# Sliding attention with its values two steps behind its scores, and three pairs of experts combined late for the second half of the tokens

## Chip, cores and metric

One core of a Trainium2 chip runs one program. The metric is the device time of one execution in microseconds (us). PE is TensorE (matmuls; PEld its weight loads), DVE is VectorE, ACT is ScalarE, POOL is GpSimd, SP is the engine that issues the DMAs here.

## The reference, cut to what matters

Two transformer blocks run one after the other on 512 tokens of width 1024, all in float32. The first mixes a convolution branch with sliding-window attention and ends with a mixture of experts; its output is normalised, and the second block begins with another normalisation.

```python
# first block
conv_o = conformer_conv(u_conv, ...) @ w_conv_out            # 31 taps per channel
attn   = sliding_window_attention(q, k, v, sinks)            # blocks of 128 queries, window 128
    scores = einsum(q, [k of block before, k of block]) * 64**-0.5 - slopes * rel
    p   = exp(scores - m);  p = p / (sum(p) + exp(sink - m));  out = einsum(p, v)
h = x + (sigmoid(gc) * conv_o + sigmoid(ga) * (attn @ w_attn_out)) @ w_out
h = h + hierarchical_moe(rms_norm(h, g_ffn), ...)            # 32 experts, 2 per token
x = rms_norm(h, g_final)
# second block
proj = rms_norm_2(x, mix_norm_gain) @ w_in_2                 # then gated delta rule, sparse attention, FFN
```

## The kernel before, in words

The program is written with tile pools. Each engine's order comes from a planner that goes by the order of the program text where it can and fills in other ready work; instructions made through `pe` (L1154) keep the text's order on PE, and `issue_after` puts an engine's instructions behind a given one. There are 20 big buffers of 8 KB a partition (`ck`, L181) and 8 PSUM banks (`ps`, L178). Float32 products are made of a high and a low part (`hilo`, L331), so a projection of one 128-column weight tile is 24 matmuls (`mm3`, L323). A weight tile is split into its parts by ACT (L196) and by POOL or DVE in turn (L214).

**Sliding attention** (`swa`, L671) goes through 8 steps, one for each block of 128 queries (`qb`) and each half of the heads (`r2`). `scores` (L681) makes the products on PE (L692), adds the bias on DVE (L694), takes the maximum (L696 to L698), lets ACT do the exponentials (L700, L702), sums (L703, L704), and scales on ACT (L706). `values` (L709) turns the result on PE (L717), copies it on ACT (L719) and multiplies by V (L722); after a block's second half, `hilo` writes the block's columns of `ath`, `atl` (L335, L336). Values of a step follow the scores of the next step. `weave` (L1368) puts one piece of `fill` after each `yield`: 20 half projections of 12 matmuls each, which are the last queries, the last convolution channel and six gate tiles (their tanh is L664). Beside it the convolution's taps (L572 on DVE, one chain a channel) are handed out four at a time by `pump`. After the attention comes `branch(ath, atl)` (L621), which reads all blocks.

**The experts** (`moe`, L983) go by 16 pairs `i`. For each: gate, turning of the pair before, half of `combine` of pair i-2, up, the rest of `combine`, and `down` of pair i-1, which writes its result to the one buffer `self.y` as high and low part (L339, L340). `combine` (L1214) multiplies by a one-hot matrix for each of 4 token tiles and 2 halves, two matmuls each, and DVE adds the result to `h` (L1225). At pair 15 a branch (`overflow`, L1057) is passed, which all engines skip here.

**The end of the first block** (`block2`, L1278): after pair 15's `combine` of a tile, `done` squares it on ACT (L1287), multiplies it by a gain (`gained`, L1291: DVE for tiles 0 and 1, POOL for 2 and 3), and squares it again. `pair` (L1293) makes the two norms' roots for two tiles at once (L1297 to L1304, root at L388) and scales each tile (L1307). `turn` (L368) transposes a tile on PE (L374) and splits it (L335, L336). `begin(2)` (L284) starts two projections on the first 256 tokens as soon as tiles 0 and 1 are turned; `finish` does the other 256. The second block (`phase_b`, L1347) takes these from `begun`. Weight tiles are prepared ahead by `fill_w` (L249), which keeps `1 + look` of them ready; `look` is 2 here.

Of the kernel before, what the change touches and what calls it, by code (L numbers as in the profile page):

```python
# [15 lines left out]
P = 128  # L16
S = 512
D = 1024
# [134 lines left out]

AHEAD = 11


class Net:
# [513 lines left out]
    def swa(self, q, kv, ath, atl):  # L671
# [9 lines left out]
        def scores(qb, r2):  # L681
            nk = 128 if qb == 0 else 256
            k0 = max(qb - 1, 0) * P
            s = self.small([P, 4, 256], "sc", bufs=2)
            mx, nmx, sm, es = (self.small([P, 4], n) for n in ("mx", "nmx", "sm", "es"))
# [41 lines left out]

        steps = [(qb, r2) for qb in range(NT) for r2 in range(2)]
        prev = None
        for st in steps:  # L730
            s = scores(*st)
            yield
            if prev is not None:
                values(*prev)
                yield
            else:
                for _ in range(3):
                    yield
            prev = st + (s,)
        values(*prev)  # L740

# [241 lines left out]
    def moe(self):  # L983

        quad, hms, ys = self.quad, {}, {}
        self.gather_first()
        self.weights()
        self.prefetch(AHEAD)
        for i in range(16):
            q = quad[i // 2]  # L990
            back = self.combine(quad[i // 2 - 1], i % 2, ys.pop(i - 2)) if i > 1 else iter(())
            if i % 2 == 0:
                g = self.gather(i // 2 + 1, quad) if i < 14 else iter(())
                next(g, None)
                self.gather_back(i // 2, quad)
            gate = self.experts("w_gate", i, q)
            if i:
                hT = self.turned(hms.pop(i - 1))
            for _ in range(2):
                next(g, None)  # L1000
            for _ in range(4):
                next(back, None)
            hms[i] = self.gated_up(gate, self.experts("w_up", i, q))
            if i % 2 == 0:
                quad[i // 2]["back"]()
            for _ in back:
# [11 lines left out]
        self.block2(quad.pop(7), y)  # L1018

# [173 lines left out]

    def down(self, i, hT, q):

# [3 lines left out]
        for jj in range(2):  # L1199
# [7 lines left out]
            self.prefetch(self.used + AHEAD)  # L1207
        y = self.y
        for half in range(2):
# [3 lines left out]

    def combine(self, q, j, y, done=None):  # L1214

        nc = self.nc
        mm = nc.tensor.matmul
        for t in range(NT):
            for half in range(2):
                fs = slice(half * 512, half * 512 + 512)  # L1220
                pc = self.ps()
                l = q["ohT"][:, j, t * P:(t + 1) * P]
                self.pe(mm, pc, l, y[:, 0, fs], start=True, stop=False)
                self.pe(mm, pc, l, y[:, 1, fs], start=False, stop=True)
# [52 lines left out]

    def block2(self, q, y):  # L1278

# [9 lines left out]
        def gained(t):  # L1289
            e = nc.gpsimd if t > 1 else nc.vector  # L1290
            e.tensor_tensor(out=self.h[:, t], in0=self.h[:, t], in1=self.rows[:, 0], op=ALU.mult)  # L1291

        def pair(t2):  # L1293

            s, v_, r_ = ss[t2], v[t2], r[t2]
            iv = self.small([P, 2], "iv")
# [16 lines left out]
        def done(t):  # L1313
            if t > 1:
                with self.tc.issue_after(first[0].ins):
                    squares(t, 0)
                gained(t)
                return
# [17 lines left out]
        for t in (2, 3):  # L1336
# [846 lines left out]
```

## Time and profile before

| | |
|---|---|
| median of 3 runs | 1784.6 us (1783.42 to 1784.62) |
| the profiled execution | 1785.45 us, of which the span is 1783.7 us |
| mean granted PE clock | 0.985 |
| PE busy | 1716.4 us (96%), 8672 matmuls |
| DVE, ACT, POOL busy | 827.6 (46%), 561.3 (31%), 332.4 us (19%) |
| attention, from its first scores to the first `branch` | 75.65 to about 172.5 us |
| experts | about 345 to 818 us |
| end of the first block, to the end of `finish` | 818 to 850 us |

The span runs from the first to the last instruction of the profiled execution; the rest of its time lies around it. Times in the rows are microseconds from the start of the span. A matmul's recorded end is modelled, so matmuls of one stream overlap: their step from start to start is what they cost. A clock of 1.00 is 2.4 GHz and 0.50 is 1.2 GHz.

### The profile page before, as it was taken

The page shows a single profiled execution, that of the slowest core. Times are in us where ns is not written, and L with a number is a line of the kernel's source. Part 1 is how long each engine was busy: PE and PEld are TensorE (multiplying, and loading weights), DVE is VectorE, ACT ScalarE, POOL GpSimd, SP SyncE. Part 2 cuts the span into 40 slices and gives each one's busy share as a digit, 9 for nine tenths or more (in the row PEclk, how much of TensorE's full clock was granted, in tenths as well). Part 3 has the DMA queues.
Part 4 walks back from the last instruction along what each step waited for, and adds up shares of the span by engine and source line. Part 5 has one row for each costly group of instructions (what it writes and reads, how often), then busy time and mean ns, then how long its engine had stood idle before and what let it go on. Part 6 is the DMA issues. An engine that isn't in the chain of part 4 may idle for free.

```text
span 1783.7 us, 21733 instructions
## 1 busy us (share of the span) xinstructions
PE 1716.4 (96%) x8672; PEld 1224.0 (69%) x8672; DVE 827.6 (46%) x1516; ACT 561.3 (31%) x1052; POOL 332.4 (19%) x208
## 2 busy tenths in 40 slices
PE   8998999999999999997999999899999899999998
PEld 6866888644444454434769988776578788888886
DVE  6996365723242333237576224556835422232222
ACT  4355254310101010104662234434523322332331
POOL 1000000000000000003327312321124133333450
PEclk9998999999999999998999999999999999999999
DMA  6221326599999999992311011210123233331431
GB/s 228 71 71 24 118 95 236 213 414 384 424 425 422 427 425 426 425 375 69 99 47 36 25 64 46 72 56 25 48 71 130 71 118 94 95 95 48 142 106 48
DMA packets 131594, 303.70 MB, mean 170 GB/s; under 512 B 5757, under 2 KB 90493, under 8 KB 106402
## 3 DMA queue, kind: packets, MB, share of 16 engines
q1 hardware_dynamic: 131490, 302.28, 45.1%
q8 instruction: 70, 1.15, 0.3%
q14 instruction: 34, 0.28, 0.0%
HBM read 300.16 MB, written 2.10 MB: 169 GB/s over the span
## 4 chain that ended last, share of the span: by engine, by line
PE 44%; DVE 5%; ACT 3%; issue 3%; POOL 1%; DVEq 0%; ACTq 0%; POOLq 0%
PE ps L327 8%; PE ps L328 8%; PE ps L329 8%; PE ps L2121 3%; PE ps L2120 3%; PE ps L2119 3%; PE ps L1607 1%; PE ps L1621 1%; PE ps L1156 1%; PE ps L1623 1%; PE ps L1926 1%; PE ps L1921 1%; PE ps L1903 1%; PE ps L1829 1%; DVE ck L1492 1%
## 5 line engine op out<-in xcount | busy, mean ns | idle before, releaser
L327 PE MATMUL ps<-ck,ck 128*128 128x512 f32 (+2 forms) x1112 | 438.0, 395 | 5.3 <-ACT ck L196 2.7
L328 PE MATMUL ps<-ck,ck 128*128 128x512 f32 (+2 forms) x1112 | 429.3, 387 | 1.1 <-DVE ck L336 1.1
L329 PE MATMUL ps<-ck,ck 128*128 128x512 f32 (+2 forms) x1112 | 427.4, 385 | 0.5 <-POOL ck L214 0.5
L327 PEld LDWEIGHTS ps<-ck,ck 128*128 128x128 f32 (+1 forms) x1112 | 210.2, 189 | 60.5 <-issue 10.2
L328 PEld LDWEIGHTS ps<-ck,ck 128*128 128x128 f32 (+1 forms) x1112 | 210.5, 189 | 48.3 <-issue 7.8
L329 PEld LDWEIGHTS ps<-ck,ck 128*128 128x128 f32 (+1 forms) x1112 | 210.4, 189 | 42.8 <-issue 1.5
L1156 PE MATMUL ps<-ck,ck 128*64 128x512 f32 x1024 | 226.3, 594 | 0.0
L214 POOL TENSOR_TENSOR ck<-ck,ck 128x512 fp32r<-128x512 f32 (+1 forms) x81 | 141.9, 1768 | 357.8 <-ACT ck L196 225.4
L1156 PEld LDWEIGHTS ps<-ck,ck 128*64 128x64 f32 x1024 | 72.0, 137 | 142.1 <-issue 135.8
L214 DVE TENSOR_TENSOR ck<-ck,ck 128x512 fp32r<-128x512 f32 (+1 forms) x109 | 110.8, 1036 | 91.1 <-PE ps L2120 44.2
L2119 PE MATMUL ps<-ck,ck 128*128 128x512 f32 x304 | 119.8, 395 | 0.0
L2121 PE MATMUL ps<-ck,ck 128*128 128x512 f32 x304 | 118.5, 390 | 0.0
L2120 PE MATMUL ps<-ck,ck 128*128 128x512 f32 x304 | 118.4, 390 | 0.0
L1156 PE MATMUL ps<-ck,hT 128*64 128x512 f32 x512 | 115.0, 602 | 2.0 <-PEq L1062 2.0
L1138 POOL TENSOR_TENSOR ohw<-oh,wt 128x512 f32<-128x512 f32 x16 | 16.5, 1050 | 470.2 <-issue 334.4
L214 POOL TENSOR_TENSOR ck<-wf,ck 128x1024 fp32r<-128x1024 f32 x28 | 77.3, 2791 | 143.4 <-ACT ck L196 143.4
L339 ACT ACTIVATE ck<-ps,ws 128x512 fp32r<-128x512 f32 x32 | 21.9, 687 | 253.9 <-PE ps L1156 253.9
L196 ACT ACTIVATE ck<-ck 128x1024 fp32r<-128x1024 f32 (+1 forms) x98 | 87.0, 911 | 13.7 <-PE ps L1921 4.2
L1156 PEld LDWEIGHTS ps<-ck,hT 128*64 128x64 f32 x512 | 36.4, 138 | 72.9 <-issue 63.0
L572 DVE SCALAR_TENSOR_TENSOR ck<-ck,wdw,ck 128x495 f32<-128x495 f32 (+23 forms) x120 | 83.8, 730 | 0.3
L1225 DVE TENSOR_TENSOR h<-h,ps 128x512 f32<-128x512 f32 x128 | 79.6, 678 | 6.9 <-PE ps L1156 6.9
L2051 DVE TENSOR_TENSOR sf<-ps,sf 128x512 f32<-128x512 f32 x22 | 15.2, 691 | 127.6 <-PE ps L329 127.6
(398 smaller groups left out, 2232.3 us busy)
## 6 DMA issues: line engine op xcount, KB each, us to landing
ck<-in_w_down SPq DMA_DIRECT2D x74, 1024.0 KB, 9.4
ck<-in_w_gate SPq DMA_DIRECT2D x64, 1024.0 KB, 11.2
ck<-in_w_up SPq DMA_DIRECT2D x64, 1024.0 KB, 9.3
ck<-in_w_in SPq DMA_DIRECT2D x34, 1024.0 KB, 5.1
wf<-in_w_gate_up SPq DMA_DIRECT2D x42, 512.0 KB, 4.8
ck<-in_w_out SPq DMA_DIRECT2D x8, 1024.0 KB, 4.9
h<-in_x SPq DMA_DIRECT2D x4, 512.0 KB, 6.5
ck<-in_w_in SPq DMA_DIRECT2D x4, 512.0 KB, 7.7
```

The costliest lines, as they stand in the source:

```text
L196: nc.scalar.activation(out=h, in_=src, func=AF.Copy)
L214: e.tensor_tensor(out=out, in0=src, in1=h.bitcast(F32), op=ALU.subtract)
L327: mm(ps, wh[:, k], xh[:, k, cols], start=k == 0, stop=False, skip_group_check=part)
L328: mm(ps, wh[:, k], xl[:, k, cols], start=False, stop=False, skip_group_check=part)
L329: mm(ps, wl[:, k], xh[:, k, cols], start=False, stop=k == K - 1, skip_group_check=part)
L339: nc.scalar.activation(out=h, in_=src, func=AF.Copy, scale=scale)
L572: nc.vector.scalar_tensor_tensor(out=y[:, c, o:], in0=v[:, c, :512 - o], scalar=wdw[:, c, 30 - o:31 - o], in1=y[:, c, o:], op0=ALU.mult, o ...
L1156: return self.tc.keep_in_program_order(f(*args, **kw))
L1225: nc.vector.tensor_tensor(out=self.h[:, t, fs], in0=self.h[:, t, fs], in1=pc, op=ALU.add)
L2119: mm(acc[t], ah[:, kk, ts], wh[:, k], start=kk == 0, stop=False)
L2120: mm(acc[t], ah[:, kk, ts], wl[:, k], start=False, stop=False)
L2121: mm(acc[t], al[:, kk, ts], wh[:, k], start=False, stop=kk == K - 1)
```

## The change

`values` of a step now come after the scores of the step after the next, and the buffer `sc` for scores has three copies instead of two. After the first step's scores four fill pieces stand as before; the last two steps of values have one fill piece between them.

The pairs 13, 14 and 15 are combined at once only for token tiles 0 and 1. Pairs 13 and 15 get result buffers of their own, and after pair 15's tiles 0 and 1 all three pairs are combined for tiles 2 and 3: six matmuls into one PSUM bank and one DVE addition for each half tile. `gained` of tiles 2 and 3 moves from POOL to DVE and behind the turning of tiles 0 and 1. `pair` computes the second norm's argument with fewer small operations. `begin` starts four projections instead of two.

```diff
+LAST = (13, 14, 15)
 def swa:
-            s = self.small([P, 4, 256], "sc", bufs=2)
+            s = self.small([P, 4, 256], "sc", bufs=3)
-        prev = None
-        for st in steps:
+        behind = deque()
+        for st in [(qb, r2) for qb in range(NT) for r2 in range(2)]:
             s = scores(*st)
             yield
-            if prev is not None:
-                values(*prev)
+            if len(behind) == 2:
+                values(*behind.popleft())
+            yield
+            if not any(st):
                 yield
-            else:
-                for _ in range(3):
-                    yield
-            prev = st + (s,)
-        values(*prev)
+                yield
+            behind.append(st + (s,))
+        values(*behind.popleft())
+        yield
+        values(*behind.popleft())
 def moe:
-            back = self.combine(quad[i // 2 - 1], i % 2, ys.pop(i - 2)) if i > 1 else iter(())
+            back = self.combine(quad[i // 2 - 1], i % 2, ys[i - 2], range(2 if i - 2 in LAST else NT)) if i > 1 else iter(())
-                ys[i - 1] = self.down(i - 1, hT, quad[(i - 1) // 2])
+                ys[i - 1] = self.down(i - 1, hT, quad[(i - 1) // 2], self.ck([P, 2, D], F32R) if i - 1 == 13 else self.y)
-        for _ in self.combine(quad[7], 0, ys.pop(14)):
+        for _ in self.combine(quad[7], 0, ys[14], range(2)):
             pass
-        y = self.down(15, hT, quad[7])
+        ys[15] = self.down(15, hT, quad[7], self.ck([P, 2, D], F32R))
+    def combine_all(self, pairs, tiles, done=None):
+        for t in tiles:
+            for half in range(2):
...
+                for i, (l, y) in enumerate(pairs):
+                    for part in range(2):
+                        self.pe(mm, pc, l[:, t * P:(t + 1) * P], y[:, part, fs], start=i + part == 0, stop=part == 1 and i == len(pairs) - 1)
                 nc.vector.tensor_tensor(out=self.h[:, t, fs], in0=self.h[:, t, fs], in1=pc, op=ALU.add)
 def block2:
-            e = nc.gpsimd if t > 1 else nc.vector
-            e.tensor_tensor(out=self.h[:, t], in0=self.h[:, t], in1=self.rows[:, 0], op=ALU.mult)
+            nc.vector.tensor_tensor(out=self.h[:, t], in0=self.h[:, t], in1=self.rows[:, 0], op=ALU.mult)
-            nc.vector.reciprocal(out=iv, in_=v_[:, 0])
-            ts_(out=v_[:, 1], in0=s[:, 1], scalar1=1.0 / D, scalar2=None, op0=ALU.mult)
-            nc.vector.tensor_tensor(out=v_[:, 1], in0=v_[:, 1], in1=iv, op=ALU.mult)
-            ts_(out=v_[:, 1], in0=v_[:, 1], scalar1=EPS, scalar2=None, op0=ALU.add)
+            ev = self.small([P, 2], "ev")
+            ts_(out=ev, in0=v_[:, 0], scalar1=EPS, scalar2=None, op0=ALU.mult)
+            nc.vector.scalar_tensor_tensor(out=v_[:, 1], in0=s[:, 1], scalar=1.0 / D, in1=ev, op0=ALU.mult, op1=ALU.add)
-            r12 = self.small([P, 2], "r12")
-            nc.vector.tensor_tensor(out=r12, in0=r_[:, 0], in1=r_[:, 1], op=ALU.mult)
+            r12 = r_[:, 1]
-        for _ in self.combine(q, 1, y, done=done):
+        for _ in self.combine(quad[7], 1, ys[15], range(2), done=done):
+            pass
+        for _ in self.combine_all([(quad[i // 2]["ohT"][:, i % 2], ys[i]) for i in LAST], range(2, NT), done=done):
             pass
...
+        with self.tc.issue_after(last[1].ins):
+            for t in (2, 3):
+                gained(t)
-        finish = self.begin(2)
+        finish = self.begin(4)
```

## Rows read from the trace of the kernel before

**Rows 1.** Busy time by stretch: PE, PEld, DVE, ACT, POOL, clock, DMA share, GB/s.

```profile
75.00:162.40 87.40, 79.94 (x380) 54.68 (x378) 83.01 (x157) 45.44 (x130) 0.00 (x0) 0.94 0.17 49
162.40:172.50 10.10, 9.36 (x41) 6.74 (x42) 0.77 (x2) 3.39 (x7) 0.00 (x0) 0.83 0.46 104
125.00:150.00 25.00, 20.04 (x91) 12.83 (x90) 23.49 (x44) 13.78 (x36) 0.00 (x0) 0.80 0.08 26
150.00:175.00 25.00, 22.59 (x107) 15.83 (x106) 11.70 (x25) 14.39 (x38) 0.00 (x0) 0.93 0.19 43
172.00:200.00 28.00, 28.00 (x125) 23.21 (x124) 8.40 (x13) 9.76 (x14) 0.00 (x0) 1.00 0.25 77
```

**Rows 2.** PE's wait for scaled scores, 70 to 190 us: in total, times, longest.

```profile
PE ps L717 <- ACT sc L706: 7.5, 3, 4.3
```

**Rows 3.** Timeline of the attention: start, duration, engine, line [idle before <- releaser].

```profile
115.00 1.14 PE L692 MATMUL ps<-ck,ck 64*128 64x256 f32 x8
...
125.67 1.28 DVE L694 SCALAR_TENSOR_TENSOR sc<-ps,ck 128x512 f32<-128x512 f32 x2
...
131.54 0.60 ACT L664 ACTIVATE sg<-ps 128x512 f32<-128x512 f32 x1 [4.84 <-PE ps L329]
...
134.22 0.16 DVE L703 TENSOR_TENSOR sm<-sm,es 128x4 f32<-128x4 f32 x1 [0.99 <-ACT es L702]
...
135.78 1.67 PE L717 MATMUL ps<-ident,sc 128*128 128x128 f32 x4 [4.28 <-ACT sc L706]
...
162.31 0.17 DVE L704 RECIPROCAL sm<-sm 128x4 f32<-128x4 f32 x1
...
168.91 0.69 DVE L336 TENSOR_TENSOR ck<-ps,ck 128x512 fp32r<-128x512 f32 x1 [6.43 <-ACT ck L335]
...
172.59 0.60 ACT L664 ACTIVATE sg<-ps 128x512 f32<-128x512 f32 x1 [3.71 <-PE ps L329]
```

**Rows 4.** Timeline of PE from 778 to 850 us.

```profile
779.11 2.12 PE L1156 MATMUL ps<-ck,ohT 128*128 128x512 f32 x8
781.15 7.09 PE L1156 MATMUL ps<-ck,ck 128*64 128x512 f32 x32
...
813.39 0.49 PE L1156 MATMUL ps<-ck,ohT 128*128 128x512 f32 x1
...
827.54 1.97 PE L374 MATMUL ps<-ident,ck 128*128 128x128 f32 x8 [9.20 <-DVE ck L1307]
830.83 1.97 PE L374 MATMUL ps<-ident,ck 128*128 128x128 f32 x8 [1.32 <-DVE ck L1307]
832.72 0.61 PE L327 MATMUL ps<-ck,ck 128*36 128x256 f32 x2
...
840.40 2.13 PE L374 MATMUL ps<-ident,ck 128*128 128x128 f32 x16
```

**Rows 5.** Busy time by stretch, columns as in the first group.

```profile
837.00:840.40 3.40, 3.40 (x30) 3.37 (x29) 2.82 (x10) 2.44 (x3) 0.00 (x0) 1.00 0.00 0
```

**Rows 6.** Timeline of DVE and POOL from 814 to 846 us.

```profile
819.21 1.22 DVE L1291 TENSOR_TENSOR h<-h,ck 128x1024 f32<-128x1024 f32 x1
...
821.68 0.16 DVE L1299 TENSOR_SCALAR b_v<-b_ss 128x2 f32<-128x2 f32 x1
...
824.05 5.64 POOL L1291 TENSOR_TENSOR h<-h,ck 128x1024 f32<-128x1024 f32 x2 [114.77 <-ACT ck L1287]
824.17 6.60 DVE L1307 SCALAR_TENSOR_TENSOR ck<-h,r,ck 128x1024 f32<-128x1024 f32 x2
...
838.84 2.48 DVE L1307 SCALAR_TENSOR_TENSOR ck<-h,r,ck 128x1024 f32<-128x1024 f32 x2
```

**Rows 7.** SP's waits from 700 to 860 us, and DMA issues from 740 to 860 us.

```profile
SPq L1811 <- DVE ck L1307: 39.8, 1, 39.8
...
ck<-in_w_in SPq DMA_DIRECT2D x5, 1024.0 KB, 8.3
```

**Rows 8.** PE's waits after 850 us: in total, times, longest.

```profile
PE ps L1537 <- DVE grow L1468: 1.6, 1, 1.6
```

More of the change, by code (lines that the diff above doesn't have):

```diff
@@ L726, in values @@
                 self.hilo(po.pop(qb).rearrange("p (r q) -> p r q", r=4), ath[:, :, qs], atl[:, :, qs])
-        steps = [(qb, r2) for qb in range(NT) for r2 in range(2)]
-        prev = None
-        for st in steps:
+        behind = deque()
+        for st in [(qb, r2) for qb in range(NT) for r2 in range(2)]:
             s = scores(*st)
             yield
-            if prev is not None:
-                values(*prev)
+            if len(behind) == 2:
+                values(*behind.popleft())
+            yield
+            if not any(st):
                 yield
-            else:
-                for _ in range(3):
-                    yield
-            prev = st + (s,)
-        values(*prev)
+                yield
[3 more added lines that the diff above has]
+        values(*behind.popleft())
     def conv_norm(self, y, total):
@@ L1011, in moe @@
             if i:
-                ys[i - 1] = self.down(i - 1, hT, quad[(i - 1) // 2])
+                ys[i - 1] = self.down(i - 1, hT, quad[(i - 1) // 2], self.ck([P, 2, D], F32R) if i - 1 == 13 else self.y)
         hT = self.turned(hms.pop(15))
-        for _ in self.combine(quad[7], 0, ys.pop(14)):
+        for _ in self.combine(quad[7], 0, ys[14], range(2)):
             pass
-        y = self.down(15, hT, quad[7])
+        ys[15] = self.down(15, hT, quad[7], self.ck([P, 2, D], F32R))
         self.start_b()
-        self.block2(quad.pop(7), y)
+        self.block2(quad, ys)
     def weights(self):
@@ L1192, in turned, with down @@
         return hT
-    def down(self, i, hT, q):
+    def down(self, i, hT, q, y):
         nc = self.nc
@@ L1207, in down @@
             self.prefetch(self.used + AHEAD)
-        y = self.y
         for half in range(2):
@@ L1212, in down, with combine @@
         return y
-    def combine(self, q, j, y, done=None):
+    def combine(self, q, j, y, tiles, done=None):
+        return self.combine_all([(q["ohT"][:, j], y)], tiles, done)
+    def combine_all(self, pairs, tiles, done=None):
         nc = self.nc
         mm = nc.tensor.matmul
-        for t in range(NT):
+        for t in tiles:
             for half in range(2):
@@ L1221, in combine @@
                 pc = self.ps()
-                l = q["ohT"][:, j, t * P:(t + 1) * P]
-                self.pe(mm, pc, l, y[:, 0, fs], start=True, stop=False)
-                self.pe(mm, pc, l, y[:, 1, fs], start=False, stop=True)
+                for i, (l, y) in enumerate(pairs):
+                    for part in range(2):
+                        self.pe(mm, pc, l[:, t * P:(t + 1) * P], y[:, part, fs], start=i + part == 0, stop=part == 1 and i == len(pairs) - 1)
                 nc.vector.tensor_tensor(out=self.h[:, t, fs], in0=self.h[:, t, fs], in1=pc, op=ALU.add)
@@ L1276, in misc_w, with block2 @@
         return w[:, 0], w[:, 1]
-    def block2(self, q, y):
+    def block2(self, quad, ys):
         nc = self.nc
@@ L1289, in gained @@
         def gained(t):
-            e = nc.gpsimd if t > 1 else nc.vector
-            e.tensor_tensor(out=self.h[:, t], in0=self.h[:, t], in1=self.rows[:, 0], op=ALU.mult)
+            nc.vector.tensor_tensor(out=self.h[:, t], in0=self.h[:, t], in1=self.rows[:, 0], op=ALU.mult)
         def pair(t2):
             s, v_, r_ = ss[t2], v[t2], r[t2]
-            iv = self.small([P, 2], "iv")
             ts_(out=v_[:, 0], in0=s[:, 0], scalar1=1.0 / D, scalar2=EPS, op0=ALU.mult, op1=ALU.add)
-            nc.vector.reciprocal(out=iv, in_=v_[:, 0])
-            ts_(out=v_[:, 1], in0=s[:, 1], scalar1=1.0 / D, scalar2=None, op0=ALU.mult)
-            nc.vector.tensor_tensor(out=v_[:, 1], in0=v_[:, 1], in1=iv, op=ALU.mult)
-            ts_(out=v_[:, 1], in0=v_[:, 1], scalar1=EPS, scalar2=None, op0=ALU.add)
+            ev = self.small([P, 2], "ev")
+            ts_(out=ev, in0=v_[:, 0], scalar1=EPS, scalar2=None, op0=ALU.mult)
+            nc.vector.scalar_tensor_tensor(out=v_[:, 1], in0=s[:, 1], scalar=1.0 / D, in1=ev, op0=ALU.mult, op1=ALU.add)
             self.rsqrt(v_, r_)
-            r12 = self.small([P, 2], "r12")
-            nc.vector.tensor_tensor(out=r12, in0=r_[:, 0], in1=r_[:, 1], op=ALU.mult)
+            r12 = r_[:, 1]
             for u in range(2):
@@ L1316, in done @@
                     squares(t, 0)
-                gained(t)
                 return
```

## The prediction

> **What bounds the kernel now.** I read the busy times by stretch first. From 75 to 162.4 us PE and DVE are both nearly full: PE 79.94 and DVE 83.01 of 87.40 us [rows 1]. The reader should see two things there. DVE has only 87.40 - 83.01 = 4.39 us of idle time, and once its work there is done it has 0.77 us of work in the next 10.1 us [rows 1]. So PE waits in this stage for an engine that has little room itself.
>
> Then PE's waits: 7.5 us in three waits, all of values (L717) for scaled scores (L706) [rows 2]. PE also ran part of the time at 1.2 GHz. A granted clock of 0.80 over 25 us is 10 us at half speed, so 5.0 us of work lost; 0.93 over the next 25 us loses 1.75 us [rows 1]. Idle and slow clock together are 7.5 + 6.75 = 14.2 us. That is the most the attention part can give.
>
> The timeline of the attention shows why the scores come late. PE finished the scores of step 4 (counted from 0) at about 116.1 us, and DVE took them up at 125.67 us, behind convolution taps. ACT then held their exponentials behind the tanh of a gate tile that PE finished at 131.5 us, DVE waited 0.99 us for them, and PE, with nothing else in its order, stood 4.28 us until 135.78 [rows 3].
>
> At the end of the experts PE is the bound: pair follows pair without a gap, 8 matmuls of `combine` taking 2.04 us from start to start (779.11 to 781.15) [rows 4]. Pair 15's combine begins at 813.39; call this E. Behind it comes a chain on ACT and DVE in which PE has nothing to do. It stands 9.20 us until tile 0 is scaled (827.54) and 1.32 us until tile 1 (830.83), `begin` starts at 832.72, and tiles 2 and 3 are turned at 840.40 [rows 4].
>
> **The attention, part by part.** No instruction is added or removed; each `values` moves behind one more step of scores and two fill pieces. A fill piece is 12 matmuls at 28.00 / 125 = 0.224 us, so 2.7 us [rows 1]. With the scores' 1.14 us [rows 3] that is 2 x 2.7 + 1.1 = 6.5 us of PE work in place of a wait of at most 4.3. The last two steps of values get one piece (2.7 us) more ahead of them, not two.
>
> What is late next is DVE. The last softmax's reciprocal ends at 162.48 (L704), and PE's order cannot bring that forward by itself [rows 3]. From L704's start to the end of the last low part (168.91 + 0.69 = 169.60) the chain through ACT, PE, ACT, PE, ACT and DVE takes 7.3 us. The first `branch` started only at 172.5, when the last gate tile was done (its tanh at 172.59) [rows 3]. After the change only one fill piece (2.7 us) is left for these 7.3 us, and it fits into the chain's pauses. With L704 unmoved, `branch` therefore starts at 169.6: a gain of 2.9 us. That is the lower end. If L704 also moves forward by all of DVE's 4.39 us of idle time, the gain is 7.3. The upper end is the 14.2 us of a PE that never waits, for which DVE would have to put the last softmax ahead of taps.
>
> I take 2.9 + three quarters of 4.39 = **6.2 us**. The idle spot I can trace (0.99 us) comes from exponentials queued behind a tanh, and both move when PE runs ahead. I leave a quarter because PE will now wait for the last steps instead and may run slowly after that. The third `sc` copy keeps the old slack, since the scores that reuse a buffer still come right after the values that free it. Nothing on SP or POOL is moved here.
>
> **The experts' end.** Pairs 13 and 14 lose the combining of two tiles each: 2 x 8 matmuls, 2 x 2.04 = 4.1 us off PE while PE is the bound. The same 16 matmuls come back behind E, into PE's idle time. Of 12 DVE additions 8 disappear; they lay beside PE work and count nothing. The new result buffers take two of the 20 `ck` buffers when few loads are left; I count that at nothing, since the last loads keep 18 buffers; the price if that cover is gone is a rival below.
>
> Behind E, in the old trace's times: `gained` of tile 1 ran at 819.21 after an addition for tile 2; without that it starts about 0.6 us sooner, and so does the second square. From there to L1307 the old chain took 821.68 to 824.17, 2.5 us; two small operations, the final product and interleaved additions go, which leaves about 1.5 us. L1307 then starts near 822.6 [rows 6].
>
> The largest term is POOL. L1307 of tiles 0 and 1 took 6.60 us for two, starting 0.12 us after POOL's `gained` of tiles 2 and 3 (5.64 us); the same two operations for tiles 2 and 3 took 2.48 us without POOL beside them [rows 6]. With `gained` off POOL I take 2.48: a gain of 4.1. Tile 1 is scaled at 822.6 + 2.5 = 825.1 instead of 830.8, so its turning and `begin` start **5.7 us** earlier, at 827.0 instead of 832.72.
>
> `begin(4)` has 96 matmuls of 256 columns. The first 48 took 832.72 to 840.40, 7.7 us, partly at 1.2 GHz; I keep that, because PE still idles before them (its work behind E ended at 827.54 - 9.20 = 818.3 and now ends 4.1 us later, at 822.4, short of tile 0's scaling). The other 48 cost 48 x 3.40 / 30 = 5.4 us [rows 4, 5]. So `begin` ends at 827.0 + 7.7 + 5.4 = 840.1, just when tiles 2 and 3 were turned before, but with 5.4 us more of projection done. I count **5.4 us** from E on. Tiles 2 and 3 (`gained` now on DVE, 2 x 1.22, one square, 1.5 of small operations, 2.48 of L1307) follow the last low part near 828.8 and end near 837: 3 us of slack. If PE's clock does not fall, up to 2.5 us more; if POOL collides again, 4.1 less (below).
>
> The second block then gets three convolution channels at once, and its short gate chain has less PE work over it. That chain already cost PE 1.6 us in one wait [rows 8]. Between nothing and 4 us I take a loss of **1.5 us**, the size of that wait.
>
> **Sum.** -6.2 - 4.1 - 5.4 + 1.5 = -14.2 us. The profiled execution took 1785.45 (span 1783.7), which would become 1771.3; it lies 0.85 above the median of 1784.6, from which I get **1770.4 us**.
>
> **The rivals.**
> A. *POOL collides all the same.* With `gained` gone, POOL takes the subtraction halves of the next weight tiles (L214) earlier, and they can lie beside L1307 of tiles 0 and 1. It depends on where ACT's copies (L196) land, before or after the squares of tile 2. The 4.1 us come back: 1774.5.
> The Trainium skill ("SBUF — State Buffer", Who interferes with whom) states that a DVE instruction with two SBUF inputs and a POOL operation that reads SBUF shut each other out, the later one blocking wholly. Any POOL operation reading SBUF would do that by this rule, so moving one away helps only if no other takes its place; the pair of times above agrees with it.
>
> B. *DVE and ACT hold the attention.* The wait moves to the last two steps of values, with a slow clock after it, and L704 does not move. For it speaks that DVE is fuller than PE [rows 1]. The gain there is 2.9 or less; with 1 us, the whole is 1784.6 - (14.2 - 5.2) = 1775.6.
>
> C. *Both gains are given back downstream.* The loads keep pace with PE through the experts, and in the second block the shorter cover over the gate chain turns into waits. Against it: PE waits little there [rows 8]. Result about 1783.
>
> D. *Slower: ACT waits for a third weight chunk.* `begin(4)` asks for five weight tiles besides the small one, because two stay ahead; the fifth needs the third 1 MB chunk of the second block's weights. Before, SP stood 39.8 us behind a load (L1811) that waited for L1307 of tile 3, and such a chunk landed 8.3 us after issue [rows 7]. If the planner keeps the chunk behind that load, it lands about 8 us after the last L1307. ACT's copy of it, if put ahead of the high parts (L335) of tiles 2 and 3, holds them, and PE behind them. It decides from a landing later than about 840 in the old times. At old time 860 (20 us) the whole is 1790. Against it: the product r12, for which that load waited, is gone, and buffers are free after E.
>
> **How the numbers follow.** The forecast has 0.56, A 0.18, B 0.13, C 0.08, D 0.05. A measurement of this kernel tells about 0.2%, 3.6 us, from no change. Forecast, A and B are faster by more than that (0.87), C is the same (0.08), D slower (0.05). The forecast's own range runs from all upper ends short of the PE-bound attention (-7.3 - 4.1 - 7.9, nothing lost: 1765.3) to 2.9 of the attention with 4 us lost (1776.2). A and B both at once give 1779.7. I let the range reach from 1763, where part of DVE's taps yield to the last softmax, to 1779.
>
> **What would show it.** Attention: L717's waits near 135 us gone, a wait left at the last two steps, the first `branch` near 166 instead of 172.5, the clock above 0.8 from 125 to 150. Experts' end: 24 matmuls right after pair 15's first 8, L1307 at 1.2 to 1.3 us each, PE's wait for tile 0 near 2 instead of 9.2 us, four projections before tile 2 is turned. L1307 at 3 us beside L214 would show A, L704 near 162 would show B, an ACT copy waiting for a weight DMA ahead of L335 would show D. The prediction is wrong if the planner reorders work elsewhere by more than these terms.

## The result, and the profile after

The changed kernel takes 1776.01 us (median of 5, 1773.22 to 1776.99) against 1784.6 us; the ratio is 0.9949 with a 95% interval of 0.9935 to 0.9962, so 9.1 us less (6.8 to 11.6) by the ratio and 8.6 by the medians. The forecast was 1770.4, 14.2 us less, in a range from 1763 to 1779. The direction was right and the time lies in the range, but 5 of the 14.2 us did not come. The execution in the profile below took 1773.22 us (span 1771.4), 2.8 less than the median; from now on runs are therefore compared by ratio, and a stage by several profiles.

Lines of the changed file stand some lower than in the one before: L572 (the taps) has become L573, L694 L695, L704 L705, L717 L718, L1156 L1160, L1225 L1232, L1291 L1297, L1307 L1311, L214 L215.

**The attention.** Busy time by stretch of the changed kernel, columns as in [rows 1] (PE, PEld, DVE, ACT, POOL, granted clock, DMA share, GB/s):

```profile
75.00:162.40 87.40, 82.82 (x410) 57.46 (x410) 82.59 (x157) 48.77 (x137) 0.00 (x0) 0.96 0.23 61
162.40:172.50 10.10, 10.10 (x46) 8.32 (x46) 3.72 (x5) 2.79 (x5) 0.00 (x0) 1.00 0.07 14
125.00:150.00 25.00, 22.84 (x118) 15.13 (x114) 25.00 (x50) 19.32 (x53) 0.00 (x0) 1.00 0.06 11
150.00:175.00 25.00, 22.70 (x101) 16.42 (x101) 11.31 (x19) 11.25 (x27) 0.00 (x0) 0.86 0.29 74
75.00:154.62 79.62, 75.05 (x376) 52.73 (x375) 79.62 (x153) 45.09 (x129) 0.00 (x0) 0.98 0.26 67
```

PE's waits there, 60 to 190 us (in total, times, longest), and the rows of the timeline around them (start, duration, engine, line, idle before and its releaser):

```profile
PE ps L723 <- ACT PT L720: 2.2, 1, 2.2
PE ps L718 <- ACT sc L707: 2.0, 1, 2.0
```

```profile
148.97 1.53 PE L718 MATMUL ps<-ident,sc 128*128 128x128 f32 x4 [2.01 <-ACT sc L707]
...
152.71 1.12 PE L723 MATMUL ps<-PT,ck 128*64 128x256 f32 x4 [2.21 <-ACT PT L720]
...
154.62 0.17 DVE L705 RECIPROCAL sm<-sm 128x4 f32<-128x4 f32 x1
...
164.71 0.60 ACT L665 ACTIVATE sg<-ps 128x512 f32<-128x512 f32 x1 [2.11 <-PE ps L330]
```

The reader should see three things. The waits near 135 us are gone, and the clock of 125 to 150 us is 1.00 instead of 0.80. Two waits, 4.2 us, are left at the values of the last steps, with a clock of 0.86 around them. And DVE has no idle time at all before the last softmax: 79.62 busy of 79.62. Its reciprocal came 7.7 us earlier (154.62 instead of 162.31), the last gate tile's tanh 7.9 (164.71 instead of 172.59).

**The experts' end.** PE from 764 to 835 us, and under it ACT, then DVE and POOL:

```profile
764.80 7.04 PE L1160 MATMUL ps<-ck,ck 128*64 128x512 f32 x32
771.77 0.66 PE L1160 MATMUL ps<-ident,hm 128*128 128x128 f32 x4
773.69 0.49 PE L1160 MATMUL ps<-ck,ohT 128*128 128x512 f32 x1 [1.26 <-ACT ck L340]
774.47 2.94 PE L1160 MATMUL ps<-ck,ohT 128*128 128x512 f32 x7 [0.29 <-DVE ck L341]
777.34 7.81 PE L1160 MATMUL ps<-ck,ck 128*64 128x512 f32 x32
...
805.04 0.49 PE L1160 MATMUL ps<-ck,ohT 128*128 128x512 f32 x1
805.83 7.95 PE L1160 MATMUL ps<-ck,ohT 128*128 128x512 f32 x31 [0.29 <-DVE ck L341]
816.76 3.42 PE L375 MATMUL ps<-ident,ck 128*128 128x128 f32 x16 [2.98 <-DVE ck L1311]
832.48 2.20 PE L375 MATMUL ps<-ident,ck 128*128 128x128 f32 x16 [0.20 <-DVE ck L1311]
```

```profile
771.91 0.60 ACT L1184 ACTIVATE sil<-ps 128x512 f32<-128x512 f32 x1 [25.66 <-PE ps L1160]
772.46 0.60 ACT L347 ACTIVATE hT<-ps 128x512 f32<-128x512 f32 x1
772.95 1.26 ACT L340 ACTIVATE ck<-ps,ws 128x512 fp32r<-128x512 f32 x2
```

```profile
815.42 2.48 DVE L1311 SCALAR_TENSOR_TENSOR ck<-h,b_r,ck 128x1024 f32<-128x1024 f32 x2
...
816.87 5.60 POOL L215 TENSOR_TENSOR ck<-ck,ck 128x1024 fp32r<-128x1024 f32 x2 [18.41 <-ACT ck L197]
...
828.00 2.40 POOL L215 TENSOR_TENSOR ck<-ck,ck 128x1024 fp32r<-128x1024 f32 x1 [5.54 <-ACT ck L197]
828.26 2.16 DVE L394 TENSOR_TENSOR nt<-b_r 128x4 f32<-128x4 f32 x1
```

In [rows 4], 8 matmuls of `combine` follow pair 15's gate matmuls and the turning of pair 14 without a gap (779.11). Here PE stands 1.26 and 0.29 us for pair 13's result, and the 40 matmuls that follow run in part at half speed (2.94 for 7, and 7.81 us for 32 where 7.09 is usual). ACT wrote that result at 772.95, 8 us after its matmuls had ended (764.8): ACT has the write queued behind pair 15's gate (L1184), whose matmuls ended at 771.8. The new buffer comes out of the weights' rotation. That the buffer was still being read until then was my first explanation; a run below tests whether the buffer is the cause, and the loads behind that run show that its readers are not. So pair 15's combine (E) starts at 805.04, 8.35 us earlier than before, of which 6.93 was there already at 763 us.

Behind E the forecast's picture holds: the scaling of tiles 0 and 1 takes 2.48 us for both instead of 6.60, PE waits 2.98 us for tile 0 instead of 9.20, and when tiles 2 and 3 come, four projections lie behind PE, which has stood still for 0.20 us only. From 820 to 950 us PE's wait for L1468's row (now L1476) is 1.6 as in [rows 8], and one is new:

```profile
PE ps L1545 <- DVE grow L1476: 1.6, 1, 1.6
PE ps L1506 <- POOL s L1505: 1.4, 1, 1.4
```

**Stage by stage.** Start times of eight instructions in the timelines, in us, as shifts against the first profile of before. The rows are ACT's first copy of keys and values (L587 before the change), ACT's copy of the convolution norm's mean (L750), DVE's first sum of the pairs' weights (L1148), its fifteenth, ACT's load of the root's table behind pair 15's low part (L1251), DVE's copy of the gate sums of the second block (L1450), ACT's first tanh of its z gates (L1646), and ACT's last product (L2074).

| | before | before again | changed | changed again | attention alone | old buffer | before, two taps |
|---|---|---|---|---|---|---|---|
| first k/v copy | 48.11 | +1.55 | -0.06 | +1.47 | +1.56 | +1.57 | +1.16 |
| convolution norm | 217.49 | +0.33 | -7.88 | -7.03 | -7.01 | -6.91 | -12.46 |
| experts, first pairs | 360.75 | +1.78 | -7.11 | -6.37 | -6.40 | -6.24 | -11.68 |
| experts, pair 14 | 763.05 | +2.09 | -6.93 | -7.61 | -6.49 | -6.25 | -11.47 |
| E | 814.21 | +2.02 | -8.32 | -8.99 | -8.06 | -11.58 | -11.54 |
| gate sums | 881.68 | +2.01 | -12.32 | -13.04 | -8.06 | -14.00 | -11.53 |
| z gates | 939.31 | +0.61 | -12.13 | -12.74 | -6.16 | -15.44 | -11.48 |
| end | 1779.25 | +0.36 | -12.23 | -10.49 | -6.23 | -12.32 | -11.10 |

### The profile page after: what moved, and what is told of

Same layout as the page of the kernel before. It is cut to its first block, busy times and chain, and to the rows that moved or that the text cites. A ratio compares the mean times of both kernels' runs of the same rounds, so it can differ in the third digit from the quotient of the medians.

```text
span 1771.4 us, 21800 instructions
## 1 busy us (share of the span) xinstructions
PE 1712.3 (97%) x8720; PEld 1224.3 (69%) x8720; DVE 820.3 (46%) x1504; ACT 561.6 (32%) x1052; POOL 327.4 (18%) x206
## 3 DMA queue, kind: packets, MB, share of 16 engines
q8 instruction: 71, 1.16, 0.3%
## 4 chain that ended last, share of the span: by engine, by line
PE 43%; DVE 5%; issue 4%; ACT 3%; POOL 1%; ACTq 0%; POOLq 0%; DVEq 0%
PE ps L328 8%; PE ps L329 8%; PE ps L330 8%; PE ps L2129 3%; PE ps L2128 3%; PE ps L2127 3%; PE ps L1615 1%; PE ps L1160 1%; PE ps L1629 1%; PE ps L1631 1%; DVE ck L1500 1%; PE ps L1929 1%; PE ps L1837 1%; PE ps L1934 1%; POOL ck L215 1%
## 5 line engine op out<-in xcount | busy, mean ns | idle before, releaser
L328 PEld LDWEIGHTS ps<-ck,ck 128*128 128x128 f32 (+1 forms) x1128 | 212.5, 189 | 58.9 <-issue 10.1
L329 PEld LDWEIGHTS ps<-ck,ck 128*128 128x128 f32 (+1 forms) x1128 | 213.0, 189 | 48.2 <-issue 9.1
L330 PEld LDWEIGHTS ps<-ck,ck 128*128 128x128 f32 (+1 forms) x1128 | 212.6, 188 | 42.2 <-issue 1.9
L1160 PE MATMUL ps<-ck,ck 128*64 128x512 f32 x1024 | 227.8, 597 | 0.0
L215 POOL TENSOR_TENSOR ck<-ck,ck 128x512 fp32r<-128x512 f32 (+1 forms) x81 | 142.8, 1780 | 375.9 <-ACT ck L197 259.9
L1160 PEld LDWEIGHTS ps<-ck,ck 128*64 128x64 f32 x1024 | 72.3, 138 | 143.6 <-issue 137.2
L215 DVE TENSOR_TENSOR ck<-ck,ck 128x512 fp32r<-128x512 f32 (+1 forms) x109 | 111.0, 1037 | 91.8 <-PE ps L2128 43.1
L1160 PE MATMUL ps<-ck,hT 128*64 128x512 f32 x512 | 113.3, 595 | 2.4 <-PEq L1066 2.4
L215 POOL TENSOR_TENSOR ck<-wf,ck 128x1024 fp32r<-128x1024 f32 x28 | 77.8, 2811 | 141.2 <-ACT ck L197 141.2
L1160 PEld LDWEIGHTS ps<-ck,hT 128*64 128x64 f32 x512 | 35.9, 137 | 72.6 <-issue 61.9
L573 DVE SCALAR_TENSOR_TENSOR ck<-ck,wdw,ck 128x495 f32<-128x495 f32 (+23 forms) x120 | 83.4, 724 | 0.3
L1232 DVE TENSOR_TENSOR h<-h,ps 128x512 f32<-128x512 f32 x120 | 75.1, 678 | 1.3 <-PE ps L1160 1.2
L1160 PE MATMUL ps<-ck,ohT 128*128 128x512 f32 x256 | 70.0, 415 | 4.5 <-ACT ck L340 2.9
```

The source lines that it names most:

```text
L215: e.tensor_tensor(out=out, in0=src, in1=h.bitcast(F32), op=ALU.subtract)
L328: mm(ps, wh[:, k], xh[:, k, cols], start=k == 0, stop=False, skip_group_check=part)
L329: mm(ps, wh[:, k], xl[:, k, cols], start=False, stop=False, skip_group_check=part)
L330: mm(ps, wl[:, k], xh[:, k, cols], start=False, stop=k == K - 1, skip_group_check=part)
L573: nc.vector.scalar_tensor_tensor(out=y[:, c, o:], in0=v[:, c, :512 - o], scalar=wdw[:, c, 30 - o:31 - o], in1=y[:, c, o:], op0=ALU.mult, o ...
L1160: return self.tc.keep_in_program_order(f(*args, **kw))
```

## The experiments

Each ratio is taken to executions of the kernel before on the same chip; "us less" is 1784.6 times the ratio's distance from 1.

| kernel | median us | ratio, 95% interval | us less |
|---|---|---|---|
| changed | 1776.01 | 0.9949 (0.9935 to 0.9962) | 9.1 |
| changed again | 1776.35 | 0.9950 (0.9936 to 0.9963) | 8.9 |
| attention alone | 1779.69 | 0.9965 (0.9953 to 0.9977) | 6.2 |
| experts alone | 1781.84 | 0.9984 (0.9975 to 0.9993) | 2.9 |
| changed, old buffer for pair 13 | 1771.81 | 0.9919 (0.9905 to 0.9932) | 14.5 |
| changed, begin(2) | 1777.13 | 0.9956 (0.9940 to 0.9972) | 7.9 |
| changed, POOL's products back | 1780.43 | 0.9971 (0.9959 to 0.9983) | 5.2 |
| changed, pair 15 alone late | 1774.79 | 0.9939 (0.9926 to 0.9953) | 10.9 |
| changed, three taps | 1773.46 | 0.9930 (0.9916 to 0.9944) | 12.5 |
| old buffer, three taps | 1769.30 | 0.9908 (0.9894 to 0.9921) | 16.4 |
| old buffer, two taps | 1763.47 | 0.9877 (0.9862 to 0.9892) | 22.0 |
| before again | 1785.15 | 0.9998 (0.9989 to 1.0008) | 0.4 |
| before, two taps | 1774.67 | 0.9940 (0.9927 to 0.9954) | 10.7 |

### Do the two parts add?

The attention's part alone is the hunk of `swa` on the kernel before; the experts' part alone is all the rest of the diff.

> The attention's part alone (values two steps behind, three score buffers); the experts and their end stay as in the kernel before. Theory: this part is worth the 7.9 us by which the work behind the attention starts earlier in the changed kernel's profile (217.49 to 209.61 for the first gate product after it), less the 0.9 us given back before the second pair of experts: 1784.6 - 7.0 = 1777.6 us. Rival (DVE and ACT hold the attention, little is gained): 2.9 us or less, 1781.7 or more. Rival (the gain is given back in the experts, where the DMA share is 1.01): within 2 us of 1784.6.

> The experts' part alone (three pairs combined at the end, products on DVE, four projections begun); the attention stays as before. Theory: in the changed kernel's profile pair 15's combine starts only 1.4 us earlier than the attention brought it, and what follows gains 3.9: 1784.6 - 5.3 = 1779.3 us. If the two parts add, their sum with the attention alone is 12 us, and the changed kernel's median (8.6 us) then has to have lost 3 to 4 us somewhere that its own profile (12.2 us) does not show. Forecast as put on record: 4.1 + 5.4 - 1.5 = 8.0, 1776.6 us. Rival (given back in the second block): 1784 us.

6.2 and 2.9 us less (4.1 to 8.4 and 1.2 to 4.5), where 7.0 and 5.3 were expected: together 9.1, which is the whole. Within these intervals the parts add. The second is the small one. In its profile too, E came only 1.35 us earlier against pair 14's row.

### The buffer of pair 13's result

```
-ys[i - 1] = self.down(..., self.ck([P, 2, D], F32R) if i - 1 == 13 else self.y)
+ys[i - 1] = self.down(..., self.ck([P, 2, D], F32R) if i - 1 == 14 else self.y)
```

> The changed kernel, but pair 13's result stays in the buffer that has always held results, and pair 14's gets the new one. Theory: in the changed kernel pair 13's result waits for a buffer out of the weights' rotation, which PE reads until the end of pair 15's gate matmuls (771.8 us); ACT writes it at 772.95 instead of about 764.2, PE stands 1.26 and 0.29 us for it and then runs 8 + 32 matmuls at half speed in part (2.94 and 7.81 us instead of 2.1 and 7.09). Without that wait 2.4 us come back: 1776.0 - 2.4 = 1773.6 us, and PE goes from pair 15's transposes into combine without a gap. Rival (the time is lost anyway, in the wait of the overflow test or for the weights' DMA): 1776.0 us, the wait of 2.4 us at the overflow test grows to about 4.

14.5 us less instead of 9: 5.5 us more by the ratios, 4.5 by the medians of that comparison, against 2.4 expected. PE in that profile:

```profile
772.44 0.66 PE L1160 MATMUL ps<-ident,hm 128*128 128x128 f32 x4
772.85 2.12 PE L1160 MATMUL ps<-ck,ohT 128*128 128x512 f32 x8
774.90 7.09 PE L1160 MATMUL ps<-ck,ck 128*64 128x512 f32 x32
784.28 7.09 PE L1160 MATMUL ps<-ck,hT 128*64 128x512 f32 x32 [2.30 <-PEq L1066]
```

The wait and the half speed behind it are gone, and the wait at the overflow test (2.30 us here, 2.41 in the changed kernel) is no longer than it was; the rival falls. From pair 15's transposes to E it takes 29.34 us (772.44 to 801.78) instead of 33.27 (771.77 to 805.04). Of these 3.9 us, 1.5 are the wait, 1.6 the combine behind it, 0.8 the matmuls after that: the wait itself is less than half of what it cost. Every profile with the new buffer for pair 13 shows the same 1.26 us.

So the buffer is the cause. How it acts is not what the expectation says. SP's last five loads of `down` weights, in the kernel before, in this run and in the changed kernel:

```profile
768.91 7.25 SPq L794 DMA_DIRECT2D ck<-in_w_down  x5
```

```profile
762.66 7.67 SPq L797 DMA_DIRECT2D ck<-in_w_down  x5
```

```profile
764.99 7.19 SPq L797 DMA_DIRECT2D ck<-in_w_down  x5
```

Counted from pair 14's sum of weights (763.05, 756.80 and 756.12) they begin after 5.86, 5.86 and 8.87 us. The loads ahead of them go out at the same places in all three. By this order pair 13's result took the buffer that the first of these five loads would have taken, and a load could go into that one 5.86 us after the landmark, at 761.98, before pair 13's `down` matmuls had ended (764.8). So it was free in time. The trace agrees: the only semaphore of a load that the late write waits for is one that no load of pair 15's gate weights uses. What held the write back was its place in ACT's order behind L1184 and L347; why the planner put it there when the buffer changed stays open.

### Pair 15 alone combined late

```
-LAST = (13, 14, 15)
+LAST = (15,)        # and results of 13 and 14 in self.y, combine of 14 over NT tiles
```

> The changed kernel, but only pair 15 is combined late for tiles 2 and 3; pairs 13 and 14 go into h as before, and their results stay in the old buffer. 16 matmuls of 0.255 us return to PE while it is the bound (4.1 us), and the wait for pair 13's buffer goes. Theory: in the changed kernel these two cancel (the attention alone brings pair 15's combine 1.6 us forward of what the pair before has, the changed kernel 1.4): 1776.2 us within 1. Forecast as put on record (nothing lost for the buffer): 1776.2 + 4.1 = 1780.3 us.

10.9 us less, 1.9 more than the changed kernel (1.2 to 1.6 by the medians), within the 1 us expected or somewhat over. The intervals of the two overlap, so combining pairs 13 and 14 late gained nothing that can be seen as it was written and may have cost 1 to 2 us; it is worth 3.6 (14.5 - 10.9; 3.0 by the medians) once the buffer is right. The profile of this run is of the longest of its five executions (1781.66 us, the others 1774.37 to 1774.90), so only times close together are taken from it. Behind E the 16 matmuls cost next to nothing, as forecast: tile 0 is turned 11.72 us after E with them (816.76 - 805.04) and 11.30 without (819.31 - 808.01).

### What the end consists of

`begin(4)` made `begin(2)`:

> The changed kernel with two projections begun in place of four before tiles 2 and 3 are turned. Theory (as forecast): the other two projections' first halves, 5.4 us of PE, no longer fill the time until tiles 2 and 3 are scaled, PE's wait there grows from 0.2 us to about 5, and the 1.5 us counted as lost in the second block come back: 1776.2 + 5.4 - 1.5 = 1780.1 us. Rival (the loss in the second block was counted where there is none): 1781.6 us. Rival (the cover was worth nothing, because PE's work only moves): 1776.2 us.

1.1 us lost by the ratios, not 3.9, and the intervals do not tell 1.1 from nothing: this lies nearest to the rival that the cover was worth nothing. In the profile PE's wait for tiles 2 and 3 grows as expected, and they are turned 25.3 us after E (831.87 - 806.55) instead of 27.4:

```profile
806.55 0.51 PE L1160 MATMUL ps<-ck,ohT 128*128 128x512 f32 x1
...
831.87 3.54 PE L375 MATMUL ps<-ident,ck 128*128 128x128 f32 x16 [3.76 <-DVE ck L1311]
```

So the longer `begin` covers 5.4 us of PE work but delays tiles 2 and 3 by 2.1, and part of the remaining 3.3 goes in the second block, where the new wait of 1.4 us for POOL is not seen in this run. From E to the z gates the gain is 1.6 us here and 3.8 in the changed kernel's two profiles.

The products of tiles 2 and 3 back on POOL, at their old place:

```
-            nc.vector.tensor_tensor(out=self.h[:, t], ...)
+            e = nc.gpsimd if t > 1 else nc.vector
+            e.tensor_tensor(out=self.h[:, t], ...)
```

> The changed kernel with the gain products of tiles 2 and 3 back on POOL, right after their additions. Theory (as forecast): POOL's two products (5.64 us before) lie beside the scaling of tiles 0 and 1 on DVE again, which takes 6.6 instead of 2.48 us; PE's wait of 2.98 us for tile 0 grows by the 4.1: 1776.2 + 4.1 = 1780.3 us. Rival (the subtraction halves of the weights collide there anyway; POOL has one of them from 816.87): 1776.2 us, the scaling at 2.5 us as now. Rival (later additions delay POOL until the scaling is under way): about 1778 us.

5.2 us less instead of 9: 3.8 lost, 4.2 by the medians, where 4.1 was forecast. Its timeline (its lines stand one lower than the changed kernel's):

```profile
815.52 4.65 POOL L1298 TENSOR_TENSOR h<-h,ck 128x1024 f32<-128x1024 f32 x2 [112.45 <-ACT ck L1294]
815.66 2.24 DVE L396 TENSOR_SCALAR nt<-nt 128x4 f32<-128x4 f32 x1
817.93 2.26 DVE L397 TENSOR_TENSOR b_r<-b_r,nt 128x4 f32<-128x4 f32 x1
820.22 3.13 DVE L1312 SCALAR_TENSOR_TENSOR ck<-h,b_r,ck 128x1024 f32<-128x1024 f32 x2
821.67 3.70 PE L375 MATMUL ps<-ident,ck 128*128 128x128 f32 x16 [7.25 <-DVE ck L1312]
```

It is not the scaling that pays this time but two operations on 4 elements a partition: each takes 2.2 us instead of 0.16, about as long as one product on POOL. So the 4.1 us came back at another place than the forecast named; the scaling itself pays 0.65 (3.13 instead of 2.48). The Trainium skill ("SBUF — State Buffer", Who interferes with whom) says that of a DVE and a POOL operation that contend the later one blocks fully; the rows of L396 and L397, each begun inside a product on POOL, agree. Not every DVE operation contends: in the changed kernel the reciprocal L390 took its usual 0.17 us inside POOL's L215 of 828.00, and L394 right behind it 2.16.

### What holds the attention

Three convolution taps a step in place of four, on the changed kernel (a step is here one `yield` in `weave`, two for each of the attention's 8 steps):

```
-self.weave([self.swa(q, kv, ath, atl)], fill, pump=4)
+self.weave([self.swa(q, kv, ath, atl)], fill, pump=3)
```

> The changed kernel with three instead of four convolution taps put on DVE at each step of the attention; the rest follow in the next stage, where DVE is less than half busy. Theory (DVE holds the attention: it has no idle time at all from 75 to the last softmax at 154.62): the last softmax comes some 5 us or more earlier, the two waits of 2.0 and 2.2 us at the last steps go, with part of the half-speed stretch behind them (0.81 from 154.62 to 162.31, 1.5 us): 1776.2 - 4.5 = 1771.7 us. Rival (PE's and ACT's order holds it): 1776.2 us, the waits stay. Rival (the taps are missed by the normalisation at the next stage's end): slower, 1779 us, with a wait for DVE near 209.

12.5 us less, 3.5 more than the changed kernel (2.6 to 2.9 by the medians), where 4.5 were expected; the wait for scaled scores is gone, one of 2.4 us for the transposed ones stays. With the old buffer as well, and then with two taps:

> The changed kernel with both remedies: pair 13's result in the old buffer (it was worth 4.4 us alone) and three convolution taps a step in place of four (2.8 alone). Theory (they lie in different stages and add): 1776.2 - 4.4 - 2.8 = 1769.0 us. Rival (what the attention gains is given back later, by a lower granted clock): 1771.8 us, as with the buffer alone.

> As the run with both remedies, but two taps a step. Theory (with three taps DVE no longer holds the attention all along; of PE's waits there one of 2.4 us is left, behind ACT's copies of the last step, which fewer taps don't shorten, and the taps left over run into the next stage): 1769 us within 1. Rival (DVE still holds it): 1767 us or less. Rival (the taps come too late for the normalisation): 1771 us or more, PE waiting for DVE near 205 us.

16.4 us less, so the two remedies add (9 + 5.5 + 3.5 = 18 expected by ratios, 16.4 within their intervals). The expectation for two taps was wrong: 22.0 us less, 1763.47 us, the best kernel of this study. I had taken a single remaining wait of 2.4 us for all there was to gain, but fewer taps also shorten it (1.1 us left). And PE is full at full clock:

```profile
125.00:150.00 25.00, 24.22 (x133) 16.65 (x132) 24.66 (x48) 19.49 (x54) 0.00 (x0) 1.00 0.04 8
150.00:175.00 25.00, 24.92 (x118) 19.40 (x117) 17.02 (x25) 7.23 (x14) 0.00 (x0) 1.00 0.29 78
```

Is the new order of the values then needed? Two taps on the kernel before, with values one step behind:

> The kernel before, values one step behind their scores as they were, with two convolution taps a step in place of four and nothing else. Theory (the 7.5 us of waits and the half-speed stretches of the attention come from taps that stand ahead of the softmax on DVE; where the values stand matters only as long as they do): the waits of 7.5 us fall below 2, the next stage starts as early as with the change, 8 us or more before 217.49, and the end gains 5 us or more: 1779.7 us or less. Rival (one step and two fill pieces are too short for the softmax's own chain of DVE, ACT, DVE and ACT, whatever DVE has besides): waits of 4 us or more stay, 1782 us or more.

10.7 us less, as much as the whole change or somewhat more. Its stretches and its one wait for scaled scores (7.5 us in [rows 2]):

```profile
125.00:150.00 25.00, 24.98 (x128) 17.69 (x128) 23.66 (x45) 16.75 (x49) 0.00 (x0) 1.00 0.00 1
150.00:175.00 25.00, 23.84 (x113) 18.48 (x113) 18.37 (x28) 9.15 (x17) 0.00 (x0) 1.00 0.35 85
```

```profile
PE ps L717 <- ACT sc L706: 1.1, 1, 1.1
```

The step between scores and values was long enough. What made it too short were taps queued ahead of the softmax on DVE, which have no hurry: with two taps a step the convolution norm still begins 12.5 us earlier. Little is then left for the new order: from the first copy of keys and values to the norm it takes 155.76 us here (49.27 to 205.03) and 154.86 in the run with the old buffer and two taps (48.57 to 203.43), which has the values two steps behind. That is 0.9 us from two single profiles, where the new order was worth 7.3 with four taps.

### Two executions of one kernel

> The changed kernel once more, unaltered. Its first profile was of the shortest of its five executions (1773.22 us, granted clock 0.990; the others 1774.55 to 1776.99 at 0.988). Theory: executions differ by where the granted clock falls to half after a wait of PE, so median 1776.0, within 1.5, and a profile nearer the median has one or two more stretches below 1.00 of 2 to 4 us lost in all, at the experts' start or at the experts' end. Rival: they differ by DMA landing times, and a wait of PE for a load is longer at an unchanged clock.

> The kernel before once more, unaltered, for a second profile of it. The attention alone moved the work behind it 8 to 8.5 us forward but the end only 4.9 us. Theory: the difference is stretches at half speed that lie elsewhere from execution to execution, 1 to 3 us each, and the second profile of before differs from its first by as much between the same landmarks, above all from 850 to 940 us (granted clock 0.97 there before, 0.95 with the attention alone). Rival: the work behind an earlier attention meets a later one (loads, POOL), and the two profiles of before agree there within 0.5 us. Median 1784.6 us.

The changed kernel repeats (1776.35). The profiles of one kernel differ by steps: before again loses 1.4 us from the norm to the first pairs and wins 1.4 from the gate sums to the z gates, against its own first profile; the changed kernel again loses 2.3 between the z gates and the end, of which its first profile shows nothing. Where the first of these steps lies, the clock tells it. The stretch from the last router work through the first expert matmuls, in before again, in before, and in the changed kernel:

```profile
334.00:361.00 27.00, 24.85 (x146) 14.08 (x145) 12.14 (x45) 7.16 (x12) 2.05 (x2) 0.94 0.67 254
```

```profile
334.00:361.00 27.00, 24.81 (x153) 14.16 (x153) 12.76 (x47) 6.61 (x12) 2.62 (x3) 1.00 0.71 276
```

```profile
326.00:354.00 28.00, 26.09 (x151) 14.95 (x152) 12.85 (x47) 6.57 (x12) 2.74 (x3) 0.94 0.68 267
```

27 x 0.06 is 1.6 us of lost work: PE pauses there for the router in every execution, and in most the granted clock falls after it. Over the 27 us that end 0.25 us behind the start of the first pairs' sum it is 0.94 in eleven of the fourteen profiles and 1.00 in three (before, experts alone, old buffer with two taps). The first profile of before is thus the exception, and the 0.8 us that the changed kernel seemed to give back from the norm to the first pairs need no effect of the change. The same goes for the 1.9 us that the attention alone loses from the gate sums to the z gates: the clock over that stretch is 0.94 in before, 0.97 in before again and 0.91 there. Why the clock falls in one execution and not in the next stays open. The 2.3 us of the changed kernel again were expected at the experts and lie elsewhere; what they are stays open.

## Why the prediction was right or wrong

**The attention: right in size, by luck, since both of its terms were wrong.** Forecast 6.2 us; 6.2 measured (4.1 to 8.4), and 7.3 at the convolution norm (the attention alone against before again, -7.01 - 0.33, with the same start). The signs it named came: no wait near 135, two waits left at the last steps, clock 1.00, first `branch` at 164.5 where 166 was said. But the 6.2 were 2.9 + 3.3. The 3.3, "three quarters" of DVE's idle time by which L704 moves, was too small: the reciprocal moved 7.7 us, 4.4 by DVE's idle time (all of it) and most of the rest, 2.8 us, because three taps and a sum fell behind the last softmax. The 2.9, by which `branch` was to follow L704 sooner, did not come: from L704 to the last gate tile's tanh it takes 10.09 us instead of 10.28. The stretches, first before the change and then after, show both, the second term by their length and the taps in DVE's column (0.86 and 3.66):

```profile
162.31:172.59 10.28, 9.45 (x41) 6.82 (x42) 0.86 (x3) 3.40 (x8) 0.00 (x0) 0.83 0.45 102
```

```profile
154.62:164.71 10.09, 10.08 (x47) 6.62 (x46) 3.66 (x7) 3.88 (x8) 0.00 (x0) 0.85 0.01 2
```

The step that failed in the second term is "only one fill piece (2.7 us) is left": the last gate tile, 24 matmuls and so two pieces, stands behind the last softmax in both kernels, and PE is full there (10.08 of 10.09 us) at a clock of 0.85. The two errors, 4.4 us too little and 2.7 too much, had opposite signs.

**The experts: the step that failed.** The forecast gave 4.1 us to 16 matmuls taken off the bound PE and counted the two new result buffers "at nothing, since the last loads keep 18 buffers". The late combining was worth 3.0 to 3.6 once the buffer was right; as built, it gained nothing that can be seen (pair 15 alone late 10.9 less, changed 9.1). The number of buffers left was the wrong question, and the rival that was to hold the price of it was not written. What the runs showed in its place: with a new buffer for pair 13's result ACT's write of it stands behind pair 15's gate, 8 us late, PE waits 1.26 and 0.29 us for it, and the path to E is 3.9 us longer, half speed included. By the order of the loads the buffer was free in time; the cost came through ACT's order, and why that order changed stays open. With this one line mended the kernel is 14.5 us less, and 14.2 were forecast, so the line accounts for the missing 5 us. That the two numbers are so close is again partly luck: 1.7 of the 14.5 are a clock that no term held (see the last section).

**Behind E: the sum right, its terms not.** Forecast 5.4 - 1.5 = 3.9; 3.8 in both profiles of the changed kernel, 4.7 by ratio (pair 15 alone late against the attention alone). The collision with POOL was sized right (4.1 forecast, 3.8 to 4.2 measured), but with the products back it falls on two small operations and not on the scaling that the forecast named. The work that `begin(4)` covers was counted as a gain on its own, but tiles 2 and 3 then come later for it; alone it is worth 1.1 us, which is not told from nothing, and not 3.9. The loss in the second block is there (a new wait of 1.4 us), at another place than the one named: L1468's stayed at 1.6.

**The rivals.** A did not happen: POOL's subtraction started at 816.87, in the scaling of tile 0 or 1, and the two still took 2.48. A later one met a small operation of tiles 2 and 3 instead (L394, 2.16 us instead of 0.16), under `begin`'s cover. B had the cause right (DVE) and the consequence wrong: L704 did move. C's loss of everything did not come; the parts add. D did not come either: ACT has no wait for a weight DMA from 740 to 870 us. What no rival held was ACT's order: a new buffer was treated as memory alone, and it moved the write of a result behind an instruction of a later pair.

## What to carry to other kernels

After moving a result to another buffer, look in the trace for the write of that result: when it starts, how long after its matmuls ended, and what stands just ahead of it on its engine. A count of the buffers that are left does not tell. Here a write 8 us late cost 4.5 to 5.5 us. Where an engine is full and another waits for it, ask first whether work without hurry stands in its queue ahead of the work that is awaited; here halving the taps per step did more (10.7 us) than reordering the consumer (6.2). And judge terms below 2 us by repeated timings, since two profiles of one kernel differ by steps of 1.4 to 2.3 us between the same two instructions.

## What the runs showed of the hardware

DVE operations on 4 elements a partition, 0.16 us by themselves, took 2.16 to 2.26 us when they began while POOL was in a product or a subtraction of 128x1024: L394 and L397, which have both inputs in SBUF, and also L396, a scalar operation with one input tile. Others did not. The reciprocal L390 of the changed kernel began 0.05 us after POOL's L215 (828.00, shown above) and took 0.17 us, and a low part (L337), which reads PSUM, took 0.69 us at 818.54 beside POOL's pair from 816.87, as the same line does without POOL:

```profile
818.54 0.69 DVE L337 TENSOR_TENSOR ck<-ps,ck 128x512 fp32r<-128x512 f32 x1 [0.64 <-ACT ck L336]
...
828.05 0.17 DVE L390 RECIPROCAL b_r<-b_r 128x4 f32<-128x4 f32 x1
```

PE's pause before the first expert matmuls ended with a granted clock of 1.00 over 27 us in one execution of the kernel before and 0.94 in another, and 0.94 in eleven of fourteen profiles. And the clock told kernels apart that differ by 8 matmuls: behind the pause of the overflow test (1.92 to 2.42 us everywhere) the next 32 matmuls took 8.78 or 8.79 us in four of the five profiles with 16 combine matmuls around pair 15's `up`, and 7.09 in all nine with 8; the granted clock over them is 0.80 in before and 1.00 in the changed kernel. For the change this is a gain of 1.7 us that its reasons did not hold; by the profiles it is part of the 3.6 above.

```profile
794.33 8.78 PE L1156 MATMUL ps<-ck,hT 128*64 128x512 f32 x32 [1.92 <-PEq L1062]
```

The row is that of before again; the one of the old buffer stands above (784.28). Why it goes this way is open.
